# Causal mask of the decay matrices: selects by index on GpSimd in place of a masking product in PSUM

## The chip, the cores and the metric

The kernel runs on one core of a Trainium2 chip. A core has a matrix engine (TensorE, PE in the profile, with its weight loads as PEld), a vector engine (VectorE, DVE), an engine for functions of one operand (ScalarE, ACT), a general engine (GpSimd, POOL) and a queue from which most transfers are issued (SyncE, SP). The metric is the time of the program on the device in microseconds; each kernel is timed in several runs and the median is given.

## The reference

One streaming step of a trunk layer: an input projection, a group of four gated-DeltaNet heads beside a pooling group, an output projection and a SwiGLU feed-forward part, over 2048 prompt frames and 64 frames of a running stream. What the change touches is the decay matrix `gamma` of a chunk, which is lower triangular:

```python
G = jnp.cumsum(g, axis=-1)
lower_incl = idx[:, None] >= idx[None, :]
lower_strict = idx[:, None] > idx[None, :]
gamma = jnp.exp(jnp.where(lower_incl, G[..., :, None] - G[..., None, :], -jnp.inf))
...
Lm = jnp.where(lower_strict, jnp.einsum('bhncd,bhnsd->bhncs', kb, k) * gamma, 0.0)
...
qk = jnp.einsum('bhncd,bhnsd->bhncs', q, k) * gamma
```

`Lm` is then inverted as a unit triangular matrix (`T`), and `T`, `qk` and the decayed keys feed a scan over the chunks.

## The kernel before, in words

The prompt is cut into four blocks of 512 frames; the 64 frames of the running stream ride along with the first. Per block the kernel projects (`pp`, fp32r products of weights split in a high and a low part, `wsp`), runs the heads and the pooling groups, and multiplies with the output projection (`pz`). When the four blocks are through, the feed-forward part runs over all frames in three passes; it is more than half of the time and has none of the changed code.

A head takes a block of 512 frames as four chunks of 128. The class `Front` prepares two chunks at a time: there are 32 fronts for the prompt (4 blocks x 4 heads x 2) and one, `s`, for the running stream, which packs two heads of 64 frames into each 128 x 128 tile. A front does the following, with the line numbers of the kernel before:

- `rowmm` (L1008) puts the running sum G, one row for all partitions, into a PSUM bank `gb`. ScalarE takes its exponential EG from it (tile `TV`); GpSimd copies the last column (`EL`), and VectorE makes `Qd`.
- A bf16 product of an identity `idbf` and a tile `negm` (0 on and above the diagonal, -1e30 below) is added onto the same bank (L1056). For `s` it is `negm2`, which also masks the block where two heads would mix. So it must wait until EG has been read.
- ScalarE takes the exponential of the masked bank with a bias per partition: the decay matrix `Gam`, zero where it is masked. Rows are the earlier frame and columns the later one.
- GpSimd subtracts the identity: `U` (tile `Gst`, L1061) is the decay without its diagonal of ones.
- TensorE multiplies keys with queries and keys (`gr`); VectorE multiplies the results with `U` and with `Gam`, in place. GpSimd adds a scaled identity `idw` to `U`, ScalarE casts it to f16 (`Wh`).
- Seven levels of small f16 products (`py`, `pt`) with level masks `lmask` on VectorE build the inverse; `pf`, `px` refine it once. The scan (`pk`, `po`) follows.

The masks and identities are made once at the start by VectorE, from a DMA of `lmask` (seven level masks and the causal one) and from the constants.

Two things set the order of the work. The program text is only recorded: every engine call becomes an operation with a rank (`Machine.note`), and `Machine.issue` lays all of them out on the five engines by a list schedule, with an estimate of each operation's duration (`Machine.cost`, L147), margins and buffer slots. That order is fixed in the program; on the chip each engine works through its own list and waits on semaphores. All instructions stand under one line, L285, where the recorded call is made, so they are told apart by the names of their tiles. And `Front.all` yields between its steps (`yield LAT_G` and the like), which sets how many products of other work are recorded between two steps of a front.

Of the kernel before, what the change touches and what calls it, by code (L numbers as in the profile page):

```python
# [10 lines left out]
BF16 = mybir.dt.bfloat16  # L11
# [3 lines left out]
ALU = mybir.AluOpType  # L15
# [3 lines left out]
P = 128  # L19
# [3 lines left out]
DEC = 64  # L23
NTOK = SEQ + DEC
C = 128
# [344 lines left out]
def hybrid_kernel(ctx, tc, a, o):  # L370
    nc = machine = Machine(tc.nc)
# [7 lines left out]
    def cost(n, dt):  # L379
        clock["pe"] += n * (1.67e-3 if dt == F32 else 0.427e-3) + 0.005  # L380

    def mm(out, lhsT, rhs, start, stop, **kw):
        nc.tensor.matmul(out, lhsT, rhs, start=start, stop=stop, **kw)
        n = 1
        for d in out.shape[1:]:
            n *= d
        cost(n, rhs.dtype)
# [55 lines left out]
    def pool(name, where=ctx, early=False, behind=False, **kw):  # L443
        return Pool(machine, where.enter_context(tc.tile_pool(name=name, bufs=1, **kw)), early, behind)
# [7 lines left out]
    cp1, gp = pool("cp1", p1, True), pool("gp", p1, True)  # L452
# [24 lines left out]
    for lo, n in S0:  # L477
        for i in range(2):
            nc.sync.dma_start(out=x0[i][:, :, lo : lo + n],
                              in_=a["xT"][4 * i : 4 * i + 4, :, lo : lo + n].rearrange("k p t -> p k t"))  # L480
# [35 lines left out]
    for j in range(NBLK):  # L516
        win = [("win", m) for m in range(21)]
        base = len(plan)
# [409 lines left out]
    ident, convw, onw, psc = names["ident"], names["convw"].rearrange("p (m t) -> p m t", t=4), names["onw"], names["psc"]  # L928
# [11 lines left out]
    selp = cp1.tile([P, 4, 1], F32R, tag="selp", name="selp")  # L940
    nc.vector.tensor_copy(selp, names["sel"].unsqueeze(2))
    lm_f = gp.tile([P, 2, YW], F32, tag="Yqk", name="lm_f", bufs=NY).rearrange("p i n -> p (i n)")[:, :1024].rearrange("p (i n) -> p i n", i=2).rearrange("p i (l n) -> p (i l) n", n=P)
    nc.sync.dma_start(out=lm_f, in_=a["lmask"])
    lmask = cp1.tile([P, 8, P], F16, tag="lmask", name="lmask")
    nc.vector.tensor_copy(lmask[:, :7], lm_f[:, :7])
    negm = cp1.tile([P, P], BF16, tag="negm", name="negm")
    nc.vector.tensor_copy(negm, lm_f[:, 7])

    negm2 = cp1.tile([P, P], BF16, tag="negm2", name="negm2")
    nc.vector.tensor_copy(negm2, lm_f[:, 7])  # L950
    nc.vector.memset(negm2[:DEC, DEC:], -1e30)
    id16 = cp1.tile([P, P], F16, tag="id16", name="id16")
    nc.vector.tensor_copy(id16, ident)
    idw = cp1.tile([P, P], F16, tag="idw", name="idw")
# [1 line left out]
    pm = bank(0, "pm")  # L956
    mm(pm[:, :P], lmask[:, 0], id16, start=True, stop=True)
    nc.scalar.copy(lmask[:, 7], pm[:, :P])
    idbf = cp1.tile([P, P], BF16, tag="idbf", name="idbf")
    nc.vector.tensor_copy(idbf, ident)  # L960

    def history(B, t, x, at, step, keep):

# [9 lines left out]
    def bc(t, nch, n):  # L973
        return t.unsqueeze(1).to_broadcast([t.shape[0], nch, n])
# [4 lines left out]
    class Front:  # L979
# [43 lines left out]
        def all(self):  # L1023
            tag, chunk = self.tag, self.chunk
# [13 lines left out]
            for c in range(2):  # L1038
# [8 lines left out]
            gb = self.ps(f"gb_{tag}")  # L1047
# [5 lines left out]
            Qd = self.Qd = gt([P, 2, C], F32, "Qd", NOUT)  # L1053
            tt(Qd, self.Yqk[:, 0, self.off : self.off + 2 * C].rearrange("p (c n) -> p c n", n=C), EG, ALU.mult)

            mm(gb[:, : 2 * C], idbf, bc(negm2 if self.h is None else negm, 2, C), start=False, stop=True,  # L1056
               skip_group_check=True)
            Gam = self.QKG = gt([P, 2, C], F32, "Gam", NOUT)
            for c in range(2):
                act(Gam[:, c], gb[:, c * C : (c + 1) * C], AF.Exp, bias=self.fall()[:, c : c + 1])  # L1060
            U = lev(F32, "Gst")  # L1061
            nc.gpsimd.tensor_tensor(out=U, in0=Gam, in1=bc(ident, 2, C), op=ALU.subtract)
            yield LAT_G
            ps = self.ps(f"gr_{tag}")
            for c in range(2):
# [52 lines left out]
            for c in range(2):  # L1118
                for i in range(2):
                    mm(px[:, c * C : (c + 1) * C], FF[:, i, c], V[:, c], start=c == i == 0, stop=i == 1,  # L1120
                       skip_group_check=c > 0)
# [416 lines left out]
    for k in (4, 5, 6, 7, 0, 1, 2, 3):  # L1538
        t = wpool.tile([P, 512], F32, tag="xc", name=f"od{k}", bufs=XBUFS["xc"])
# [23 lines left out]
    for nm in FH[3:]:  # L1563
        t = f2.tile([P, 4, 2, N2], F32R, tag=f"h{nm}", name=f"hB{nm}")
        hq[nm] = [t[:, k] for k in range(4)]
    fill = Chain(load_h(0, FH[3:]))
# [194 lines left out]
    for op in order:  # L1761
        b = op[1]
        if op[0] == "gu":
# [18 lines left out]
            if f == NF - 1 and b + 1 < NB2:  # L1782
                nxt.finish()
                fill = Chain(load_h(b + 1, FH))
# [63 lines left out]
def _layout(inp):  # L1848
    import numpy as np

    g = {k: np.asarray(v) for k, v in inp.items()}
    f32 = np.float32
    r = {}
    xp, xs = g["x_prompt"][0], g["x_sample"][0]
    xa = np.concatenate([xp[: PB[0]], xs, xp[PB[0] :]], axis=0)
    r["xT"] = xa.T.reshape(KT, P, NTOK)
    col = lambda w: w.reshape(-1, P).T
    r["nw"] = np.concatenate([col(g["norm1_w"][0]), col(g["norm2_w"][0]), col(g["normf_w"])], axis=1)
    w = g["w_in"][0]

    def tiles(w):
        K, M = w.shape
        return w.reshape(K // P, P, M // P, P).transpose(2, 1, 0, 3).reshape(M // P, P, K)

    ab = np.zeros((D, P), f32)
    ab[:, 0:4] = w[:, 2048:2052]
    ab[:, 32:36] = w[:, 2052:2056]
    ab[:, 64:] = ab[:, :64]
    cols = [ab]
    for h in range(NH):  # L1870
        for i in range(4):
            cols.append(w[:, (4 * i + h) * P : (4 * i + h + 1) * P])
    cols.append(w[:, 2056:])
    r["win"] = tiles(np.concatenate(cols, axis=1))
    r["wout"] = tiles(g["w_out"][0])
    r["wg"], r["wu"] = tiles(g["w_gate"][0]), tiles(g["w_up"][0])

    wd, f0, rows = g["w_down"][0].reshape(NF, P, D), 0, []
    for G in FGROUPS:
        rows += [f0 + i for i in (*range(0, G, 2), *range(1, G, 2))]  # L1880
        f0 += G
    r["wd"] = tiles(wd[rows].reshape(NF * P, D))
    c = {}
    c["convw"] = g["conv_w"][0].reshape(4, 12, P).transpose(2, 1, 0)
    c["onw"] = g["onorm_w"][0].reshape(P, 1)
    c["psc"] = col(g["pool_scale"][0])
    c["poolw"] = g["pool_w"][0].transpose(2, 0, 1)
    c["alog"] = np.zeros((P, 1), f32)
    c["alog"][0:4, 0] = g["a_log"][0]
    c["dtb"] = np.zeros((P, 1), f32)  # L1890
    c["dtb"][0:4, 0] = g["dt_bias"][0]
    c["sconv"], c["spool"] = np.zeros((P, 12, 2, 3), f32), np.zeros((P, 4, 2, HP), f32)
    c["sconv"][:, :, 1] = g["state_conv"][0, 0].T.reshape(12, P, 3).transpose(1, 0, 2)
    c["spool"][:, :, 1] = g["state_pool"][0, 0].T.reshape(4, P, HP).transpose(1, 0, 2)
    c["sdelta"] = g["state_delta"][0, 0].transpose(1, 0, 2)

    c["sgn"] = np.ones((P, 1), f32)
    c["sgn"][32:64] = c["sgn"][96:] = -1.0
    c["ident"] = np.eye(P, dtype=f32)
    i = np.arange(P)  # L1900
    lm = np.zeros((P, 8, P), f32)
    for l in range(7):
        s = 1 << l
        lm[:, l, :] = (i[:, None] == i[None]) * 1.0 - ((i[:, None] // (2 * s) == i[None] // (2 * s)) & (i[:, None] // s > i[None] // s))
        lm[:, l, :] /= WSCALE
    lm[:, 7, :] = np.where(i[None] >= i[:, None], 0.0, -1e30)
    r["lmask"] = lm
    z = np.zeros((P, 12), f32)
    for t in range(3):
        for h in range(4):  # L1910
            z[32 * t + h, 4 * t + h] = 1.0
    c["sel12"] = z
    z = np.zeros((P, 4), f32)
    for h in range(4):
        z[h, h] = 1.0
        z[32 + h, h] = 1.0
    c["sel"] = z
    z = np.zeros((P, 4, 16), f32)
    for gi, win in enumerate(WIN):
        z[:, gi, :] = 1.0 / np.minimum(win, np.arange(16) + 1)  # L1920
    c["pcnt"] = z
    r["consts"] = np.concatenate([c[nm].reshape(P, w).astype(f32) for nm, w in CONSTS], axis=1)
    return {k: np.ascontiguousarray(v) for k, v in r.items()}
# [32 lines left out]
```

## Time and profile before

| | |
|---|---|
| median of 3 runs | 2296.41 us (2295.73 to 2298.98) |
| span of the profiled execution | 2295.8 us |
| instructions | 41549 |
| data moved | 536.96 MB |
| first part, with the heads | about 0 to 905 us |
| feed-forward part | from there to the end |

The span is what the profile shows of one execution, from its first to its last instruction. Matrix products are pipelined: the row of a product gives its length from entry to exit, and the next one starts earlier than it ends. Names such as `gb_p` are tiles, with `_p` for the prompt and `_s` for the running stream.

### The profile page before, as it was taken

Reading aid. Unit: us, or ns where it says so; the run is one execution under the profiler, and the core shown is the slowest. Engines: PE = TensorE matmul, PEld = TensorE weight load, DVE = VectorE, ACT = ScalarE, POOL = GpSimd, SP = SyncE. Lnnn points to the kernel's source line nnn. Section 1 sums busy time; section 2 is a strip of 40 time slices with the busy share of each in tenths; the row PEclk is TensorE's granted clock in tenths of the full one; section 3 lists DMA queues with packets and bytes.
Section 4 is the critical chain, followed back from the end, with each engine's and each line's share of the span. In section 5 each row is a group of like instructions: output and inputs, shape, how many; then the busy total and the mean of one; then the engine's idle time right before and its main releaser. Section 6 shows DMA issues by size and latency. Waiting matters only on the chain.

```text
span 2295.8 us, 41549 instructions
## 1 busy us (share of the span) xinstructions
PE 2271.8 (99%) x14518; PEld 2132.1 (93%) x14518; DVE 1711.3 (75%) x3129; ACT 1342.1 (58%) x3039; POOL 833.4 (36%) x893
## 2 busy tenths in 40 slices
PE   8999999999999999999999999999999999999998
PEld 8898898888787888999999999999999999999998
DVE  8989876685678896788888786866667768666576
ACT  6986866684769864565446366554334574353344
POOL 3425342453247450565434236622111453010112
PEclk9999999999999999999999999999999999999999
DMA  8755586578476767866776578778765776666653
GB/s 295 263 182 193 199 294 234 191 238 277 159 245 232 212 212 254 304 247 247 272 260 238 185 264 292 248 266 302 234 198 199 263 271 230 209 216 224 210 195 103
DMA packets 256514, 536.96 MB, mean 234 GB/s; under 512 B 30000, under 2 KB 94000, under 8 KB 256304
## 3 DMA queue, kind: packets, MB, share of 16 engines
q1 hardware_dynamic: 255728, 533.58, 69.3%
q8 instruction: 114, 1.87, 0.3%
q14 instruction: 96, 0.79, 0.1%
q10 hardware_dynamic: 576, 0.72, 0.1%
HBM read 403.62 MB, written 130.58 MB: 233 GB/s over the span
## 4 chain that ended last, share of the span: by engine, by line
PE 88%; DVE 5%; DMA 3%; ACT 2%; issue 1%; POOL 1%; SPq 0%; DVEq 0%; POOLq 0%; ACTq 0%
PE px L285 21%; PE pp L285 17%; PE pz L285 13%; PE py L285 10%; PE dx L285 8%; PE dy L285 4%; PE d L285 3%; PE dz L285 2%; PE pk_p L285 2%; PE pt_p L285 2%; PE gr_p L285 1%; DVE y L285 1%; PE py_p L285 1%; DVE h L285 1%; DMA hpd<-xt 1%
## 5 line engine op out<-in xcount | busy, mean ns | idle before, releaser
L285 PE MATMUL pp<-h,wsp 128*128 128x512 f32 (+1 forms) x2480 | 547.9, 364 | 10.0 <-DVE wsp L285 10.0
L285 PEld LDWEIGHTS pp<-h,wsp 128*128 128x128 f32 x2480 | 401.4, 189 | 58.2 <-ACT wsp L285 9.2
L285 ACT CAST ws<-wr 128x512 fp32r<-128x512 f32 x198 | 122.1, 618 | 166.7 <-PE dx L285 55.2
L285 DVE TENSOR_TENSOR ws<-wr,ws 128x512 fp32r<-128x512 f32 x198 | 173.4, 879 | 30.9 <-ACT ws L285 27.1
L285 POOL TENSOR_TENSOR q<-hr,hr 128x352 f32<-128x352 f32 x52 | 58.0, 1116 | 369.6 <-DVE hr L285 366.8
L285 ACT CAST wsd<-wrd 128x512 fp32r<-128x512 f32 (+1 forms) x120 | 62.6, 526 | 174.8 <-PE dx L285 66.8
L285 DVE TENSOR_TENSOR y<-y,dx 128x352 f32<-128x352 f32 x240 | 121.8, 517 | 57.0 <-PE dx L285 56.0
L285 PE MATMUL pz<-op,wsp 128*128 128x288 f32 (+1 forms) x768 | 163.0, 353 | 0.0
L285 PE MATMUL px<-hA,ws 128*128 128x352 f32 x792 | 145.2, 322 | 0.0
L285 ACT ACTIVATE hr<-g 128x352 f32<-128x352 f32 x132 | 65.6, 497 | 133.7 <-DVE g L285 133.5
L285 PE MATMUL py<-hA,wsS 128*128 128x352 f32 x792 | 141.5, 322 | 2.0 <-DMA wsS<-gS 1.6
L285 PE MATMUL py<-hB,wsS 128*128 128x352 f32 x792 | 141.7, 322 | 0.0
L285 PE MATMUL pz<-hB,ws 128*128 128x352 f32 x792 | 141.0, 322 | 0.0
L285 ACT CAST TV_p<-pt_p 128x512 f16<-128x512 f32 x192 | 110.4, 589 | 49.6 <-PE pt_p L285 49.2
L285 PE MATMUL px<-hA,wsS 128*128 128x352 f32 x792 | 138.5, 322 | 0.0
L285 PE MATMUL px<-hBT,wsS 128*128 128x352 f32 x792 | 137.9, 322 | 0.2 <-ACT g L285 0.2
L285 PE MATMUL px<-hBT,ws 128*128 128x352 f32 x792 | 137.7, 322 | 0.0
L285 PEld LDWEIGHTS pz<-op,wsp 128*128 128x128 f32 x768 | 120.9, 188 | 12.1
L285 PEld LDWEIGHTS py<-hA,wsS 128*128 128x128 f32 x792 | 129.4, 188 | 2.6 <-DMA wsS<-gS 1.9
L285 PEld LDWEIGHTS px<-hA,ws 128*128 128x128 f32 x792 | 130.0, 188 | 0.1
L285 PE MATMUL dy<-hq,wsdS 128*128 128x352 f32 x672 | 129.6, 322 | 0.0
L285 PEld LDWEIGHTS py<-hB,wsS 128*128 128x128 f32 x792 | 129.4, 188 | 0.0
(697 smaller groups left out, 5777.2 us busy)
## 6 DMA issues: line engine op xcount, KB each, us to landing
wsS<-gS SPq DMA_DIRECT2D x176, 512.0 KB, 4.5
wsp<-wnd SPq DMA_DIRECT2D x126, 512.0 KB, 3.8
gS<-wsS SPq DMA_DIRECT2D x88, 512.0 KB, 4.9
wsdS<-dsd SPq DMA_DIRECT2D x88, 512.0 KB, 4.4
wr<-in_wg_dram SPq DMA_DIRECT2D x132, 256.0 KB, 3.5
wnd<-wsp SPq DMA_DIRECT2D x42, 512.0 KB, 5.0
wrd<-in_wd_dram SPq DMA_DIRECT2D x68, 256.0 KB, 2.7
xd<-x2d SPq DMA_DIRECT2D x96, 176.0 KB, 4.1
```

The costliest lines, as they stand in the source:

```text
L285: getattr(getattr(self.nc, op.eng), name)(*args, **kw)
```

## The change

The masking product, its two mask tiles and the bf16 identity are left out, and the load of the masks brings seven tiles in place of eight. ScalarE takes the exponential of the unmasked bank. In place of the subtraction, GpSimd makes two selects by index: `U` takes `Gam` where the column is above the row and 0 elsewhere (so no diagonal), and then `Gam` is rewritten in place with 0 where the column is below the row. For the front `s` each select is followed by a memset of the block where the two heads would mix.

```diff
-    nc.sync.dma_start(out=lm_f, in_=a["lmask"])
+    nc.sync.dma_start(out=lm_f[:, :7], in_=a["lmask"])
     lmask = cp1.tile([P, 8, P], F16, tag="lmask", name="lmask")
     nc.vector.tensor_copy(lmask[:, :7], lm_f[:, :7])
-    negm = cp1.tile([P, P], BF16, tag="negm", name="negm")
-    nc.vector.tensor_copy(negm, lm_f[:, 7])
-
-    negm2 = cp1.tile([P, P], BF16, tag="negm2", name="negm2")
-    nc.vector.tensor_copy(negm2, lm_f[:, 7])
-    nc.vector.memset(negm2[:DEC, DEC:], -1e30)
...
-    idbf = cp1.tile([P, P], BF16, tag="idbf", name="idbf")
-    nc.vector.tensor_copy(idbf, ident)
...
-            mm(gb[:, : 2 * C], idbf, bc(negm2 if self.h is None else negm, 2, C), start=False, stop=True,
-               skip_group_check=True)
             Gam = self.QKG = gt([P, 2, C], F32, "Gam", NOUT)
             for c in range(2):
                 act(Gam[:, c], gb[:, c * C : (c + 1) * C], AF.Exp, bias=self.fall()[:, c : c + 1])
             U = lev(F32, "Gst")
-            nc.gpsimd.tensor_tensor(out=U, in0=Gam, in1=bc(ident, 2, C), op=ALU.subtract)
+            for t, op in ((U, ALU.is_gt), (Gam, ALU.is_ge)):
+                nc.gpsimd.affine_select(out=t, in_=Gam, pattern=[[0, 2], [1, C]], compare_op=op, fill=0.0, base=0, channel_multiplier=-1)
+                if self.h is None:
+                    nc.gpsimd.memset(t[:DEC, :, DEC:], 0.0)
...
-    lm = np.zeros((P, 8, P), f32)
+    lm = np.zeros((P, 7, P), f32)
...
-    lm[:, 7, :] = np.where(i[None] >= i[:, None], 0.0, -1e30)
```

The layout of the lists is made anew from the changed operations, so the first part is ordered differently throughout; behind it the lists agree. Three places follow. In VectorE's list at the start of the program, where the constants are made, the kernel before has this (`wsp_3_147` is the split of projection weights, `consts` the folded pooling weights):

```order
L285 CAST selp<-consts 128x4
L285 CAST lmask<-lm_f 128x896
L285 CAST negm<-lm_f 128x128
L285 CAST negm_159<-lm_f 128x128
L285 MEMSET negm_159 64x64
L285 CAST id_160<-consts 128x128
L285 TENSOR_SCALAR idw<-consts 128x128
L285 CAST idbf<-consts 128x128
L285 TENSOR_SCALAR consts<-consts 128x128
L285 TENSOR_TENSOR wsp_3_147<-wrp_3_146,wsp_3_147 128x512
```

and the changed kernel this:

```order
L285 CAST selp<-consts 128x4
L285 CAST lmask<-lm_f 128x896
L285 CAST id_158<-consts 128x128
L285 TENSOR_SCALAR idw<-consts 128x128
L285 TENSOR_SCALAR consts<-consts 128x128 x4
L285 TENSOR_TENSOR wsp_3_147<-wrp_3_146,wsp_3_147 128x512
```

Four operations are gone ahead of the split, and the three later ones of the four on `consts` have moved ahead of it.

In TensorE's list at the first two fronts (`p_0_0` and `p_0_1` of the first head, first block) the kernel before has:

```order
L285 MATMUL gb_p_0_0_231<-Ghl_169,selp 128x256
L285 MATMUL pp_7_0_254<-h_0_116,wsp_8_204 128x288 x10
L285 MATMUL pp_7_288_255<-h_0_115,wsp_8_202 128x288 x2
L285 LDWEIGHTS idbf
L285 MATMUL gb_p_0_0_231<-negm,idbf 128x256
L285 MATMUL po_p_0__409<-Qd_p_0_0_233,Sp 128x128
L285 MATMUL gb_p_0_1_240<-Ghl_169,selp 128x256
L285 MATMUL pp_7_288_255<-h_0_115,wsp_8_202 128x288 x10
L285 MATMUL pp_7_288_255<-h_0_116,wsp_8_204 128x288 x2
L285 LDWEIGHTS idbf
L285 MATMUL gb_p_0_1_240<-negm,idbf 128x256
L285 MATMUL gr_p_0_0_245<-Yqk_0_178 128x256 x2
```

and the changed kernel:

```order
L285 MATMUL gb_p_0_0_228<-Ghl_166,selp 128x256
L285 MATMUL pp_7_0_247<-h_0_116,wsp_8_201 128x288 x11
L285 MATMUL pp_7_288_248<-h_0_115,wsp_8_199 128x288 x4
L285 MATMUL gr_p_0_0_249<-Yqk_0_175 128x256 x2
L285 MATMUL po_p_0__409<-Qd_p_0_0_230,Sp 128x128
L285 MATMUL gb_p_0_1_237<-Ghl_166,selp 128x256
```

The two mask products and their weight loads are gone, and `gr` of the first front stands 15 `pp` products behind its row product, where it stood behind 24 of them, two masks and two further products. In ScalarE's list at the same place the exponential EG (`TV_p_0_0`) and the decay matrix now stand side by side, with nothing of other work between:

```order
L285 ACTIVATE TV_p_0_0_227<-gb_p_0_0_228 128x256
L285 ACTIVATE Gam_p_0_0_231<-gb_p_0_0_228,EC_167 128x128 x2
L285 ACTIVATE ktl_p_0_1_234,kn_p_0_1_233<-ptk_p_0_1_235 128x128
L285 ACTIVATE ktl_p_0_1_234<-ptk_p_0_1_235,EC_167 128x128 x2
L285 ACTIVATE kn_p_0_1_233<-kn_p_0_1_233,epsc 128x2
```

In the kernel before the `ktl`, `kn` and one `E` row stood between the two. GpSimd's list at these fronts had:

```order
L285 COPY EL_p_0_0_232<-TV_p_0_0_230 128x2
L285 TENSOR_TENSOR Gst_p_0_0_235<-Gam_p_0_0_234,consts 128x256
L285 COPY EL_p_0_1_241<-TV_p_0_1_239 128x2
L285 TENSOR_TENSOR Gst_p_0_1_244<-Gam_p_0_1_243,consts 128x256
L285 TENSOR_TENSOR Gst_p_0_0_235<-Gst_p_0_0_235,idw 128x256
```

and has:

```order
L285 COPY EL_p_0_0_229<-TV_p_0_0_227 128x2
L285 AFFINE_SELECT Gst_p_0_0_232<-Gam_p_0_0_231 128x256
L285 AFFINE_SELECT Gam_p_0_0_231<-Gam_p_0_0_231 128x256
L285 TENSOR_TENSOR Gst_p_0_0_232<-Gst_p_0_0_232,idw 128x256
L285 COPY EL_p_0_1_238<-TV_p_0_1_236 128x2
L285 AFFINE_SELECT Gst_p_0_1_241<-Gam_p_0_1_240 128x256
L285 AFFINE_SELECT Gam_p_0_1_240<-Gam_p_0_1_240 128x256
```

Each subtraction has become two selects, and the addition of `idw` to the first front has moved ahead of the second front's rows.

## The prediction

> **What bounds the kernel now.** I read the page first, for the engine on which the time is spent, and then the stages, to see where that engine has to wait.
>
> ```profile
> span 2295.8 us, 41549 instructions
> PE 2271.8 (99%) x14518; PEld 2132.1 (93%) x14518; DVE 1711.3 (75%) x3129; ACT 1342.1 (58%) x3039; POOL 833.4 (36%) x893
> PE 88%; DVE 5%; DMA 3%; ACT 2%; issue 1%; POOL 1%; SPq 0%; DVEq 0%; POOLq 0%; ACTq 0%
> ```
>
> The reader is to see one engine that is never free: TensorE (PE) is busy 99% of the span, 88% of the chain that ended last is its own work, and its clock is granted in full (the column 1.00 of the next rows). VectorE (DVE) is three quarters full, GpSimd (POOL) a little over a third. So a product taken off TensorE is worth its place in TensorE's queue, and a microsecond added to GpSimd costs nothing until somebody waits for it.
>
> The changed code runs in the first part alone (the last mask product starts at 812.9 us). The stages of that part, in the columns PE, PEld, DVE, ACT, POOL, then the granted clock, the share of the DMA engines and GB/s:
>
> ```profile
> 0.00:50.00 50.00, 39.71 (x282) 39.05 (x283) 39.68 (x90) 33.93 (x78) 19.75 (x32) 1.00 0.83 294
> 50.00:100.00 50.00, 49.71 (x391) 46.15 (x390) 46.41 (x92) 43.03 (x112) 20.59 (x27) 1.00 0.72 252
> 200.00:250.00 50.00, 48.98 (x318) 38.49 (x317) 45.81 (x94) 39.15 (x104) 23.26 (x31) 1.00 0.62 209
> 400.00:500.00 100.00, 100.00 (x621) 81.61 (x620) 76.81 (x151) 72.88 (x181) 48.96 (x68) 1.00 0.60 207
> ```
>
> TensorE has gaps at the start (10.3 us, before and around its first weights) and about 1 us at 200 to 250 us; in the rows between and behind it has next to none. In the first 300 us VectorE is the next engine, with 46.41 and 45.81 of 50 us. GpSimd has half its time free in each of these rows. From 900 us on the order of instructions is the same in both kernels, and nothing there enters the sum.
>
> **The change, part by part.** *The mask products.* There are 32 of them on heads of the prompt and one on the sample, and one weight load for each.
>
> ```profile
> L285 PE MATMUL gb_p<-negm,idbf x32: 269/282/286, 62.7 to 812.9; 128*128 128x256 bf16 x32
> 62.72 0.28 PE L285 MATMUL gb_p<-negm,idbf 128*128 128x256 bf16 x1
> 62.84 0.39 PE L285 MATMUL po_p__409<-Qd_p,Sp 128*128 128x128 f32 x2
> 64.79 0.28 PE L285 MATMUL gb_p<-negm,idbf 128*128 128x256 bf16 x1
> 64.91 1.03 PE L285 MATMUL gr_p<-Yqk 128*128 128x256 f32 x4
> 699.07 0.28 PE L285 MATMUL gb_p<-negm,idbf 128*128 128x256 bf16 x1
> 699.10 0.48 PE L285 MATMUL pp<-h,wsp 128*128 128x512 f32 x1
> 699.42 0.28 PE L285 MATMUL gb_p<-Ghl,selp 128*128 128x256 f32 x1
> 699.53 1.77 PE L285 MATMUL pp<-h,wsp 128*128 128x512 f32 x7
> 701.15 0.28 PE L285 MATMUL gb_p<-negm,idbf 128*128 128x256 bf16 x1
> ```
>
> The 282 ns are the length of one from entry to exit; products overlap, so what one costs is the distance from its start to the next start. That is 0.12 us twice (62.72 to 62.84, 64.79 to 64.91). At 699.07 the next product starts 0.03 us later but then holds the queue 0.32 us, while the seven behind it take (701.15 - 699.53) / 7 = 0.23 each: 0.03 + 0.09 = 0.12 again. For 31 of the 33 that makes 31 x 0.12 = **3.7 us**. The other two stand together:
>
> ```profile
> 201.60 0.31 PE L285 MATMUL gb_p<-Ghl,selp 128*128 128x256 f32 x1
> 201.98 0.27 PE L285 MATMUL gb_s<-negm,idbf 128*128 128x256 bf16 x1
> 202.44 0.27 PE L285 MATMUL gb_p<-negm,idbf 128*128 128x256 bf16 x1 [0.19 <-ACT TV_p L285]
> 202.70 0.49 PE L285 MATMUL pk_p<-vn_p,ktl_p 128*128 128x128 f32 x2
> ```
>
> A mask has to wait until ScalarE (ACT) has read the bank that it adds to (`TV_p`, the exponential EG, is what released the second). From 201.98 to 202.70 TensorE's queue holds nothing but these two: **0.7 us** more.
>
> *The constants.* The two mask tiles and the bf16 identity are made by VectorE at the start, right ahead of a weight split for which TensorE waits:
>
> ```profile
> 18.84 0.97 DVE L285 CAST negm<-lm_f 128x128 bf16<-128x128 f32 x2
> 19.57 0.62 ACT L285 CAST wsp<-wrp 128x512 fp32r<-128x512 f32 x1 [0.50 <-DMA wnd<-wsp]
> 19.88 0.11 DVE L285 MEMSET negm<- 64x64 bf16 x1
> 20.62 0.83 DVE L285 CAST idbf<-consts 128x128 bf16<-128x128 f32 x1
> 21.57 2.50 DVE L285 TENSOR_TENSOR wsp<-wrp,wsp 128x512 fp32r<-128x512 f32 x2
> 22.92 1.98 PE L285 MATMUL pp<-h,wsp 128*128 128x288 f32 x13 [0.78 <-DVE wsp L285]
> 24.06 0.66 DVE L285 TENSOR_SCALAR consts<-consts 128x128 f32<-128x128 f32 x3
> ```
>
> VectorE loses 0.97 + 0.11 + 0.83 = 1.91 us there. The new order puts the three small products of 24.06 (0.66 us) into that place, so the split can start 1.25 us sooner, at 20.3. What is late next is ScalarE's cast of the same weights, done at 19.57 + 0.62 = 20.2: it does not hold the split up. The whole wait of TensorE, 0.78 us, goes: **0.8 us**. The load of the masks, which becomes an eighth smaller, I cost at nothing: no wait of the trace ends on it, and a smaller one lands no later.
>
> *The selects.* One subtraction on GpSimd becomes two selects per front (33 subtractions, 66 selects, and two small memsets for the sample). No row shows a select, so I bound it from both sides:
>
> ```profile
> L285 POOL MEMSET wsp<- 128x256 f32 x2 | 0.6, 312 | 0.3 <-POOLq L1938 0.3
> L285 POOL TENSOR_TENSOR Gst_p<-Gam_p,consts x32: 719/742/1242, 63.9 to 814.3; 128x256 f32<-128x256 f32 x32
> L285 POOL TENSOR_TENSOR pw<-pw 128x591 f32<-128x591 f32 x1 | 1.9, 1852 | 0.1
> ```
>
> Writing 256 columns with nothing read took 0.31 us; the subtraction on the same tile took 0.74 in the middle, up to 1.24; the longest elementwise row of the list, more than twice as wide, took 1.85. A select reads one tile and writes one, with an index to compare in between. I take **0.75 us**, the row that it replaces, and keep 0.31 and 1.85 as ends. GpSimd's work then grows by 33 x (1.5 - 0.74) = 25 us, in a part where it is free half of the time. What counts is the chain. For the first front:
>
> ```profile
> 60.92 0.39 PE L285 MATMUL gb_p<-Ghl,selp 128*128 128x256 f32 x1 [0.28 <-ACT ktl_p L285]
> 61.14 1.74 PE L285 MATMUL pp<-h,wsp 128*128 128x288 f32 x12
> 61.36 0.40 ACT L285 ACTIVATE TV_p<-gb_p 128x256 f32<-128x256 f32 x1
> 63.18 0.68 ACT L285 ACTIVATE Gam_p<-gb_p,EC 128x128 f32<-128x128 f32 x2
> 63.93 0.74 POOL L285 TENSOR_TENSOR Gst_p<-Gam_p,consts 128x256 f32<-128x256 f32 x1 [1.66 <-ACT Gam_p L285]
> 66.22 0.60 DVE L285 SCALAR_TENSOR_TENSOR Gst_p<-gr_p,kn_p,Gst_p 128x128 f32<-128x128 f32 x2
> 66.74 0.41 DVE L285 TENSOR_TENSOR Gam_p<-gr_p,Gam_p 128x256 f32<-128x256 f32 x1
>   DVE Gst_p L285: 0.6, 1
> ```
>
> EG ends at 61.76 and the decay matrix Gam only starts at 63.18, because the mask comes between. In the new order of ScalarE the two stand next to each other: Gam would run 61.76 to 62.44, and the selects, 0.08 us later as at 63.93, end at 62.5 + 0.75 and 62.5 + 1.5 = 64.0. The subtraction now ends at 64.67. So the pair is done sooner than the one it replaces, as long as a select takes under 1.07 us. But the new order also spends this: it puts the products `gr` on TensorE 15 `pp` behind the row product of 60.92, and 12 `pp` took 61.14 to 62.72, 0.132 each: 61.14 + 15 x 0.132 = 63.1, where they stood at 64.91. VectorE multiplied Gam 1.83 us behind `gr` (66.74 - 64.91), so it would now ask for it at 64.9. The second select is in time up to (64.9 - 62.5) / 2 = 1.2 us. The last row, from the waits on this tile, says that VectorE stood once in 32 fronts for GpSimd's subtraction, 0.6 us; behind a late select would stand VectorE's products with the level masks, for which TensorE's next level waits. At 0.75 I cost this at **0.3 us** in all, for the fronts whose `gr` comes closest; with a select of 0.31 it would be nothing.
>
> *A rule to weigh.* The Trainium skill (GPSIMD Engine Reference, 3.1) speaks against this edit: data-dependent branching costs about 12 cycles per element there, while 4.1 calls one-input operations roughly line-rate. By the 1.2 GHz of that page an estimate for 256 columns is 2.6 us by the one and 0.2 us by the other; no row here shows which applies to a select. With the first the sum would turn into the slow rival below, with the second only its 0.3 us would go.
>
> *The sum.* 3.7 + 0.7 + 0.8 - 0.3 = 4.9 us off the profiled execution's 2295.8, that is 2290.9. The median of the runs shown, 2296.41, lies 0.6 above this span, so I predict **2291.5 us**.
>
> **The rivals.** *Given back where VectorE sets the pace.* Cut at 300 us, the view of the mask tiles has this row on prompt heads, and the one of the sample at 202.0:
>
> ```profile
> L285 PE MATMUL gb_p<-negm,idbf x11: 269/282/286, 62.7 to 286.3; 128*128 128x256 bf16 x11
> ```
>
> So 12 of the 33 masks stand where VectorE is busy 46.41 and 45.81 of 50 us. If TensorE reaches VectorE's results sooner there and only waits for them, the 12 slots (1.2 for ten, 0.7 for the pair) and the 0.8 at the start come to nothing: 4.9 - 2.7 = 2.2 us are left, 2294.2. For it speaks that the new order moves `gr` and all that follows on VectorE forward; against it, that the page has only 1 us of idle TensorE at 200 to 250. The Trainium skill (SBUF — State Buffer, section on the two separate sides) adds a reason: a GpSimd operation and a VectorE one with two SBUF inputs exclude each other for their whole length. The subtraction's spread of 719 to 1242 ns above agrees with that, and 25 us more of GpSimd would hold VectorE up a little more often.
>
> *A slow select.* The order is fixed when the program is built, so an engine that is late stops its queue. Above 1.2 us per select the first front's Gam comes late by twice the excess, and the 32 fronts together lose 64 times the excess if TensorE gets all of it. It decides from 1.2 + 4.9 / 64 = 1.3 us on. At 1.45 us, between the slowest subtraction (1.24) and the longest row (1.85), it costs 64 x 0.25 = 16 us: 2296.4 - 4.9 + 16 = 2307.5. For it: no row of a select, and a spread of the subtraction that reaches 1.24. Against it: the middle row is 0.74, and a select reads one input less.
>
> *The change does not do what it says.* The masks could have come back in another form. The order that the front shows has no `idbf` or `negm` left at its places and two selects where the subtraction stood, so I give this 2 in 100; it would be 2296.4.
>
> **How the numbers follow.** Forecast 62 in 100, with a range of its own of 2289.0 to 2294.0; rival on VectorE 20; slow select 16; no change in fact 2. What a measurement of this kernel can tell from no change is about 0.2%, 4.6 us, so faster begins at 2291.8, in the upper middle of the forecast's range: 38 of its 62 lie below it: faster 0.38. The other 24, the 20 of VectorE's rival and the 2 of no change are within 0.2%, less 1 for a VectorE that loses more than it was given: 0.45. Slower is that 1 and the slow select: 0.17. The range: its low end allows 3.5 us beyond the sum, for a cheap select and an order that happens to wait less, 2288.0; its high end takes in the second rival and the slow select up to 1.35 us (64 x 0.15 - 4.9 = 4.7 above 2296.4), 2301.0. Left out are most of the slow select, some 13 in 100, and 6 in 100 below.
>
> **What would show it.** Right: no bf16 product in the list of TensorE; the start of `pp` at 22.92 without its wait for VectorE; TensorE's busy time in 50 to 850 us shorter by about 4 us and no new row in TensorE's waits that ends on VectorE or GpSimd for more than a few tenths; selects of 0.3 to 1.0 us. Wrong: selects above 1.2 us with VectorE's product Gam waiting for GpSimd in most fronts; or stages before 300 us that take as long as now, with new TensorE gaps that VectorE ends; or a moved DMA issue for which TensorE waits, which I have at nothing, as the list of SyncE keeps its loads and only shifts them by a few places.

## The result, and the profile after

The changed kernel takes **2302.39 us** (median of 20 runs, 2298.96 to 2307.96), the kernel before in the same comparison 2297.23 us (20 runs, 2295.73 to 2301.12): a ratio of 1.0020 (95% interval 1.0014 to 1.0027). It is 5 us slower, where 5 us faster was forecast, and it lies above the forecast range (2288.0 to 2301.0). The profiled execution spans 2301.2 us against 2295.8.

The head of the page, of the changed kernel:

```profile
span 2301.2 us, 41494 instructions
PE 2273.9 (99%) x14485; PEld 2128.3 (92%) x14485; DVE 1705.2 (74%) x3125; ACT 1341.3 (58%) x3039; POOL 830.2 (36%) x928
```

The 33 products are gone (14518 to 14485) and VectorE has four operations less. GpSimd has 35 instructions more and is busy *less* than before (833.4). Busy times do not show where 5 us went; the stages do. The same stages as in the prediction, and one of 3.4 us inside the third:

```profile
0.00:50.00 50.00, 40.89 (x289) 40.38 (x290) 39.09 (x89) 34.73 (x81) 18.95 (x33) 1.00 0.84 298
50.00:100.00 50.00, 49.71 (x401) 46.80 (x400) 44.28 (x89) 43.12 (x113) 24.02 (x31) 1.00 0.71 246
200.00:250.00 50.00, 47.92 (x294) 38.22 (x294) 43.91 (x81) 32.41 (x69) 19.95 (x24) 0.97 0.63 205
400.00:500.00 100.00, 98.34 (x604) 78.56 (x602) 74.14 (x149) 71.23 (x176) 44.69 (x68) 1.00 0.60 195
235.50:238.90 3.40, 3.40 (x10) 2.55 (x9) 2.51 (x6) 0.00 (x0) 0.00 (x0) 0.50 0.64 199
```

Up to 100 us the changed kernel is ahead (289 and 401 products in the first two rows, where 282 and 391 stood). At 200 to 250 us it does 24 products fewer than before, TensorE idles 2.1 us instead of 1.0, and the granted clock, 1.00 in every row of before, is 0.97: the last row shows why, 3.4 us at exactly half clock. At 400 to 500 us there is 1.7 us of idle time that was not there. TensorE's first product of the feed-forward part starts at 938.17 us, where it started at 933.03: nearly the whole loss is made before that part.

What TensorE waited for up to 910 us (waiting tile, what ended the wait, us in total, times, longest):

```profile
PE pp L285 <- DVE wsp L285: 9.1, 2, 8.7
PE pc L285 <- DVE Rt L285: 2.0, 3, 1.1
PE pp L285 <- DVE h L285: 1.0, 3, 0.6
PE px_p L285 <- DVE TV1F_p L285: 0.6, 1, 0.6
PE os_p__2169 L285 <- DVE lo_p__2171 L285: 0.5, 1, 0.5
PE pk_p L285 <- DVE Sp L285: 0.5, 1, 0.5
PE pf_s L285 <- ACT TV_s L285: 0.5, 1, 0.5
```

In the kernel before, the first row reads 10.0 and no other row has more than 0.3. Of these rows all but the last end on VectorE, and the largest new one on `Rt`, the running sum that opens each block, for whose products `pc` TensorE stands three times (0.70, 0.24 and 1.07 us).

### The profile page after: what moved, and what is told of

Same layout as the page of the kernel before. It is cut to its first block, busy times and chain, and to the rows that moved or that the text cites. A ratio compares the mean times of both kernels' runs of the same rounds, so it can differ in the third digit from the quotient of the medians.

```text
span 2301.2 us, 41494 instructions
## 1 busy us (share of the span) xinstructions
PE 2273.9 (99%) x14485; PEld 2128.3 (92%) x14485; DVE 1705.2 (74%) x3125; ACT 1341.3 (58%) x3039; POOL 830.2 (36%) x928
## 4 chain that ended last, share of the span: by engine, by line
PE 87%; DVE 6%; DMA 3%; ACT 2%; issue 1%; POOL 0%; SPq 0%; DVEq 0%; ACTq 0%; POOLq 0%
PE px L285 20%; PE pp L285 16%; PE pz L285 13%; PE py L285 10%; PE dx L285 9%; PE dy L285 4%; PE d L285 3%; PE dz L285 2%; PE pk_p L285 2%; PE pt_p L285 2%; PE gr_p L285 1%; DVE y L285 1%; PE py_p L285 1%; DVE h L285 1%; DVE Rt L285 1%
## 5 line engine op out<-in xcount | busy, mean ns | idle before, releaser
L285 PEld LDWEIGHTS px<-hA,wsS 128*128 128x128 f32 x792 | 128.9, 188 | 0.9 <-ACT g L285 0.9
```

The lines of the kernel that those rows point to most:

```text
L285: getattr(getattr(self.nc, op.eng), name)(*args, **kw)
```

## The experiments

The kernel before was timed again beside each group of kernels, and its median moved (2297.23 to 2299.55), so each kernel is compared with the runs of before that were taken beside it. The ratios and intervals are estimated from the runs and are not the quotients of the medians, from which they differ by up to 0.0006. "Old list" is the order of the kernel before, "own" the one laid out from the changed operations with the constants as they were.

| label | work and list | median | before | difference | ratio (95% interval) |
|---|---|---|---|---|---|
| the change | changed, own list | 2302.39 | 2297.23 | +5.2 | 1.0020 (1.0014 to 1.0027) |
| e1_old_order | changed, old list | 2298.78 | 2299.55 | -0.8 | 0.9996 (0.9987 to 1.0005) |
| e3_selects_only | masks and selects, old list | 2298.24 | 2299.55 | -1.3 | 0.9997 (0.9988 to 1.0006) |
| b_lat473 | before, LAT_G 4.73 | 2297.72 | 2299.55 | -1.8 | 0.9998 (0.9989 to 1.0006) |
| a_lat473 | changed, LAT_G 4.73 | 2301.86 | 2299.55 | +2.3 | 1.0012 (1.0004 to 1.0021) |
| n_filled | changed and 33 idle products, own list | 2307.13 | 2299.13 | +8.0 | 1.0035 (1.0022 to 1.0048) |
| n_tv210 | changed, LAT_TV 2.1 | 2297.14 | 2299.13 | -2.0 | 0.9995 (0.9986 to 1.0004) |
| n_g603 | changed, LAT_G 6.03 | 2300.72 | 2299.13 | +1.6 | 1.0009 (1.0001 to 1.0018) |
| b_tv210 | before, LAT_TV 2.1 | 2296.38 | 2299.13 | -2.8 | 0.9987 (0.9978 to 0.9996) |
| n_rtwait | changed, own list, GpSimd waits at `Rt` 1, 2 | 2301.33 | 2298.60 | +2.7 | 1.0010 (1.0001 to 1.0019) |
| n_tv_xd | changed, LAT_TV 2.1, later `xd` | 2294.25 | 2298.60 | -4.4 | 0.9982 (0.9973 to 0.9991) |
| b_tv_xd | before, LAT_TV 2.1, later `xd` | 2297.78 | 2298.60 | -0.8 | 0.9996 (0.9988 to 1.0005) |
| g_tv_xd | changed, list of b_tv_xd | 2293.81 | 2298.60 | -4.8 | 0.9979 (0.9971 to 0.9988) |
| n_rt3 | n_rtwait, and `Rt` 3 | 2299.03 | 2297.90 | +1.1 | 1.0005 (0.9997 to 1.0014) |
| n_best | n_tv_xd, GpSimd waits at `Rt` 2, 3 | 2292.75 | 2297.90 | -5.2 | 0.9978 (0.9969 to 0.9987) |

### Is it the work or the order?

Two theories stood at the start: the selects or the missing masks cost something of themselves, or the new order does. *e1_old_order* makes the whole change but keeps the order of the kernel before: the old operations are laid out as if they were there, and those that the change removes are then not issued. *e3_selects_only* keeps the masks too and replaces only the subtraction.

```diff
+            machine.ghost = True
             mm(gb[:, : 2 * C], idbf, bc(negm2 if self.h is None else negm, 2, C), start=False, stop=True,
                skip_group_check=True)
+            machine.ghost = False
...
-            nc.gpsimd.tensor_tensor(out=U, in0=Gam, in1=bc(ident, 2, C), op=ALU.subtract)
+            for t, op in ((U, ALU.is_gt), (Gam, ALU.is_ge)):
+                nc.gpsimd.affine_select(out=t, in_=Gam, pattern=[[0, 2], [1, C]], compare_op=op, fill=0.0, base=0, channel_multiplier=-1)
```

> The whole change (masks, mask tiles and bf16 identity gone, selects in place of the subtraction), but the lists of all engines laid out as in the kernel before: the removed operations are planned and not issued, the selects stand where the subtraction stood. Theory A, the loss is the new layout of the lists: this kernel keeps the gain, about 2292.5 us (3.7 + 0.7 + up to 0.8 off 2297.2). Theory B, the selects hold VectorE up wherever they stand: about as slow as the changed kernel, 2301 to 2303.

> The masking products stay and the selects take the place of the subtraction, in the old layout of the lists (the selects then find their zeros already there). Theory A: no change, 2296.5 to 2298, since the pair takes 0.8 us where the subtraction took 0.74. Theory B: 2300 or more.

*b_lat473* and *a_lat473* lay out the kernel before and the changed one with `LAT_G = 4.73` in place of 4.53.

> The kernel before with the constant LAT_G at 4.73 in place of 4.53: the same work, another layout of the lists. Theory A1, any new layout of this program comes out a few us worse than the one of before: 2299 to 2305. Theory A2, the layout of the changed kernel is bad for a reason of its own (fronts packed closer): this one stays at 2296 to 2298.

> The changed kernel with LAT_G at 4.73: the same work as the changed kernel, another layout. A1: anywhere between 2292 and 2306, on average 4 to 5 us under other layouts of the kernel before. A2: 2301 to 2304 again.

The selects cost nothing: e3_selects_only is at 0.9997. Their rows in the changed kernel, found under the tiles they write (least, median and greatest ns, first and last start):

```profile
L285 POOL TENSOR_SCALAR_AFFINE_SELECT Gst_p<-Gam_p x32: 399/407/928, 61.3 to 826.1; 128x256 f32<-128x256 f32 x32
L285 POOL TENSOR_SCALAR_AFFINE_SELECT Gam_p<-Gam_p x32: 406/408/997, 61.7 to 826.5; 128x256 f32<-128x256 f32 x32
```

At 0.41 us each, two selects last about as long as the one subtraction (0.74). But e1_old_order gains only 0.8 us, within its uncertainty, which is the number of neither theory, and the changed kernel stays slow in a second order of its own (a_lat473), while the kernel before does not mind its own second order (b_lat473). The 2301.86 us of a_lat473 lie in the range of its theory A2, but the kernel before beside it was 2.3 us slower than beside the change; by the difference, +2.3, it lies between its two theories. So there are two questions: why freed slots bring nothing in the old list, and why the new list costs 5 us.

In e1_old_order TensorE runs ahead of the kernel before up to 500 us. It gives that back at 530 to 570 us (two waits of 0.9 us in all for a load of weights, one of 0.5 for ScalarE) and, the larger part, at 797 to 808 us. One row of VectorE and one of TensorE from there (the recorded call is line 298 in this kernel):

```profile
802.17 0.59 DVE L298 SCALAR_TENSOR_TENSOR xd<-xd,nw,r 128x352 f32<-128x352 f32 x1 [4.54 <-DMA xd<-x2d]
803.74 0.49 PE L298 MATMUL pk_p<-rhs_p,X_p 128*128 128x128 f32 x2 [2.47 <-DVE rhs_p L298]
```

`xd` are rows of the trunk that are loaded to prepare the feed-forward part; the first products on them stand in the last block of the first part, from about 758 us on, the last ones at 1615 us. No head needs them, but VectorE takes its list in order, so while it stands 4.54 us for a late load, everything of the heads behind it stands too. The kernel before stands 3.15 us for a load of `xd` there too, at 804.5, and TensorE has other work meanwhile. In e1_old_order TensorE's clock is then at half for 3.4 us (804.7 to 808.2). e3_selects_only, which keeps the masks, stands there too: in its profile VectorE waits 4.44 us for `xd` (to 806.86) and TensorE 1.91 us behind it, at full clock. So freed slots are not needed for this stall.

### Do freed slots count at all?

*n_filled* takes the changed kernel's lists word for word and puts a product of a mask's size back behind each row product, into the unused half of the bank.

```diff
             self.rowmm(gb)
+            machine.ride = True
+            nc.tensor.matmul(gb[:, 2 * C : 4 * C], id16, bc(lmask[:, 0], 2, C), start=True, stop=True, skip_group_check=True)
+            machine.ride = False
```

> The changed kernel with its lists exactly as they are, and 33 products of TensorE put back where the masks could have stood: right behind each row product, an f16 product of 128 x 128 by 256 columns into the unused half of the same bank, which nobody reads and nobody waits for. Same time on TensorE as a mask (0.12 us each, 3.9 us in all), without the mask's waits. If freed slots shorten the program in this list, as the prediction's sum has it, filling them again costs 3.9 us: about 2306. If TensorE is paced by what it waits for in this list, filling them costs nearly nothing: 2302 to 2303.

It is 8.0 us over the kernel before, 2.8 more than the change, from five runs and with intervals that overlap; in the profiles its feed-forward part starts 3.8 us later than that of the change (942.0 against 938.2). So the slots count in this list, the masks' removal is worth something near what the prediction said, and the new list loses some 8 us elsewhere. *n_tv210*, *n_g603* and *b_tv210* look at other lists (`LAT_TV = 2.1` in place of 2.0, `LAT_G = 6.03` in place of 4.53).

> The changed kernel with LAT_TV 2.1 in place of 2.0: the same operations in another order. Theory of the list (the constants had been chosen for the old operations, and the list that they give for the new ones is a poor one among many): another list is several us better, 2293 to 2298. Theory of the shorter hop (without the mask every front goes from its row product to gr sooner, so every list of the changed operations runs into waits for VectorE): 2300 or more, as the two lists so far (2302.4 and 2301.9).

> The changed kernel with LAT_G 6.03 in place of 4.53, a third other order, in which more of other work is recorded between the steps of a front. Theory of the list: 2293 to 2299, below the two lists so far. Theory of the shorter hop: 2300 or more.

> The kernel before with LAT_TV 2.1: the other side of n_tv210. If the changed operations are worth something once both are laid out by the same new constant, n_tv210 comes out 2 to 5 us below this one. Theory of the list: this one is within 2 us of the kernel before or worse by a few, since nothing is removed; theory of the shorter hop: it is 3 us or more below n_tv210.

Both theories are partly right. One list of the changed operations is 7 us better than the other (+5.2 and -2.0), and lists of the kernel before differ too (0, -1.8, -2.8). But with the same constants the changed operations are not ahead in any of these three pairs: +5.2 against 0, +2.3 against -1.8, -2.0 against -2.8. n_g603 falls on the side of the shorter hop, n_tv210 on the side of the list. b_tv210 meets none of its expectations: it is 2.8 us below the kernel before, and n_tv210 came out 0.8 above it.

Both new lists of the changed operations stall in the last block. In n_g603 it is GpSimd that stands, 5.43 us for a transfer, at a sum on `xd` for the feed-forward part (to 796.92); ScalarE and then TensorE stand behind it, TensorE for 3.56 us, and the half clock follows. In n_tv210 it is VectorE, as in e1_old_order. The profile of n_tv210 is that of the slowest of its eleven runs (2301.19 us, where the median is 2297.14); by their mean granted clock seven of them had no stretch at half clock (0.999; the profiles with such a stretch have 0.9978 to 0.9984, those without 0.9985 to 0.9992). Of n_tv210, VectorE, then TensorE, then the stages on both sides of TensorE's return (PE, PEld, DVE, ACT, POOL, clock, DMA share, GB/s):

```profile
804.35 1.46 DVE L285 SCALAR_TENSOR_TENSOR xd<-xd,nw,r 128x352 f32<-128x352 f32 x1 [2.94 <-DMA wsp<-wnd]
806.07 0.33 DVE L285 SCALAR_TENSOR_TENSOR Sp<-Sp,EL_p,pk_p 128x128 f32<-128x128 f32 x1
806.46 0.59 PE L285 MATMUL pk_p<-Sp,Yqk 128*128 128x128 f32 x2 [2.57 <-DVE Sp L285]
803.20:806.70 3.50, 0.93 (x7) 0.48 (x6) 2.35 (x5) 0.92 (x4) 1.21 (x2) 1.00 0.94 320
806.80:810.00 3.20, 3.20 (x17) 2.54 (x15) 1.35 (x5) 1.30 (x5) 1.14 (x3) 0.50 0.31 102
```

The name of the load in the first row is that of the transfer that ended last in the profile; the operand is `xd`. In the 3.5 us of TensorE's wait the DMA engines are 94% busy, which fits loads that are late because the transfers are full there. `Sp` behind it has nothing to do with `xd`. And behind the gap TensorE runs at half clock, 3.4 us in all, which adds 1.7 us to the 2.6 of the wait.

### The two repairs

*n_tv_xd* and *b_tv_xd* let the layout take the loads of `xd` as landing 2.5 us later, so VectorE's product on them goes further back in its list. This holds for every load of `xd`, those of the feed-forward part too: the lists are others from about 760 us up to 1650 us. *g_tv_xd* is e1_old_order's edit made on the lists of b_tv_xd.

```diff
         late = SLACK if q.eng == "tensor" and p.eng != "sync" and q.order > self.second else 0.0
+        if p.eng == "sync" and q.eng == "vector" and p.tiles and p.tiles[0].startswith("xd"):
+            late += XD
...
+XD = 2.5
-LAT_TV = 2.0
+LAT_TV = 2.1
```

*n_rtwait* aims at the `Rt` waits. The rows of VectorE and GpSimd around the start of the second block, in the changed kernel:

```profile
230.12 2.33 DVE L285 TENSOR_TENSOR_SCAN Rt<-ones,Rt 4x128 f32<-4x128 f32 x4
230.47 0.90 POOL L285 TENSOR_TENSOR prdn<-prdn 128x256 f32<-128x256 f32 x1
231.45 0.73 POOL L285 TENSOR_TENSOR prdn<-consts,prdn 128x256 f32<-128x256 f32 x1
232.25 0.64 POOL L285 TENSOR_TENSOR consts<-prdn,consts 128x256 f32<-128x256 f32 x1
232.48 1.54 DVE L285 TENSOR_SCALAR Rt<-Rt 4x128 f32<-4x128 f32 x4
232.97 0.78 POOL L285 TENSOR_TENSOR consts<-consts 128x256 f32<-128x256 f32 x1
233.03 0.61 PE L285 MATMUL pc<-consts,Rt 128*128 128x12 f32 x4 [0.70 <-DVE Rt L285]
```

and the corresponding ones of the kernel before:

```profile
226.87 1.35 DVE L285 TENSOR_TENSOR_SCAN Rt<-ones,Rt 4x128 f32<-4x128 f32 x4
229.02 0.67 DVE L285 TENSOR_SCALAR Rt<-Rt 4x128 f32<-4x128 f32 x3
229.37 1.01 PE L285 MATMUL pc<-consts,Rt 128*128 128x12 f32 x8
229.63 0.73 POOL L285 TENSOR_TENSOR prdn<-prdn 128x256 f32<-128x256 f32 x1 [2.05 <-DMA prdn<-in_wd_dram]
```

`prdn` are sums of down-projection weights that GpSimd prepares for the feed-forward part. In the kernel before their load lands just behind the running sum; in the changed one they run beside it, and four scans take 2.33 us instead of 1.35. n_rtwait makes GpSimd wait for the last row of `Rt` in blocks 1 and 2 (the second and the third, as blocks are counted from 0) by a copy of one column; in the first part nothing else moves in any engine's list.

```diff
+        if j in RTWAIT:
+            machine.after[RTWAIT[j]] = f"Rt{j}_", tick[64:68], Rt[64:68, YW - 1 : YW]
...
+RTWAIT = {1: "prdn4_0", 2: "prdn8_1"}
```

> The changed kernel with its lists as they are, and two copies of one column on GpSimd that wait for the last row of the running sum (Rt) of blocks 1 and 2, ahead of the sums of down weights (prdn) that ran beside these rows. Theory (VectorE's eight Rt rows take 4.3 us instead of 2.66 because GpSimd's two-input operations run beside them, so TensorE waits 0.95 and 1.10 us at pc, and the first of these waits is followed by 3.4 us of half clock): the rows take 2.7 us, both waits go, with them the half clock at 235 us, and the time is 2 to 4 us below the changed kernel: 1 to 3 us above the kernel before on the same chip. Rival (the waits only move to the next point where VectorE is late): 5 us above the kernel before, as the change itself.

> The changed kernel with LAT_TV 2.1 and a layout that takes the loads of xd (last block, at 770 to 900 us) to land 2.5 us later than before, so that VectorE's product on them stands further back in its list; up to about 770 us the lists are those of n_tv210. Theory (in the last block the transfers set the pace: VectorE stands 2.9 us at xd, TensorE behind it 2.6 us, and the half clock follows): that wait goes, and with it 2 to 4 us of n_tv210's time; 4 to 6 us below the kernel before. Rival (the wait is that of one execution, or comes back behind the next load): as n_tv210, 2 us below the kernel before.

> The kernel before with the same two constants as n_tv_xd. If loads of xd that are late cost the masks' kernel as much: 1 to 3 us below b_tv210, 4 to 5 below the kernel before. If the masks' kernel loses nothing there, as its profile says (3.15 us of VectorE's wait without a wait of TensorE): as b_tv210, 2 to 3 below the kernel before.

> The lists of b_tv_xd, with the masking products and their constants left out of them and the two selects in the subtraction's place: e1_old_order once more, on lists in which xd has 2.5 us more to land. If e1_old_order gained nothing because TensorE, once ahead, stood longer for the late loads and lost the clock there, the freed slots now show: 3 to 4.5 us below b_tv_xd. If freed slots are given back wherever TensorE gets ahead: within 1 us of b_tv_xd.

In n_rtwait the running sum is as fast as in the kernel before, and GpSimd's copy and sum come behind it:

```profile
231.51 1.35 DVE L288 TENSOR_TENSOR_SCAN Rt<-ones,Rt 4x128 f32<-4x128 f32 x4
232.88 0.87 DVE L288 TENSOR_SCALAR Rt<-Rt 4x128 f32<-4x128 f32 x4
233.56 0.96 PE L288 MATMUL pc<-consts,Rt 128*128 128x12 f32 x8
233.88 0.97 POOL L286 COPY tick<-Rt 4x1 f32<-4x1 f32 x1 [1.99 <-DVE Rt L288]
234.93 1.18 POOL L288 TENSOR_TENSOR prdn<-prdn 128x256 f32<-128x256 f32 x1
```

TensorE no longer waits at `pc`, its clock is full from 12 to 2292 us, and 10 of 11 runs have a mean granted clock of 0.999, where 13 of 20 of the changed kernel have 0.998 (a stretch of 3.4 us at half clock takes 0.0007 off the mean; the kernel before, whose profile has none, also has 0.998 in 10 of the 33 runs taken here, so some of its runs may have one). The time falls from +5.2 to +2.7, as the theory had it, though the two intervals overlap.

The other repair goes with a kernel faster than before. n_tv_xd, with the lists of n_tv210 up to about 760 us, is 2.4 us below it, has no wait of TensorE over 0.5 us from 50 to 910 us, and is faster than the kernel before by 0.9 to 2.7 in a thousand. b_tv_xd gains nothing by it. Its second expectation foresaw that, but put it 2 to 3 us below the kernel before; it is 0.8 below, and 2 us above b_tv210. The profiles, one execution each, show where this goes. At the first product of the feed-forward part n_tv_xd is 7.4 us ahead of n_tv210 (930.1 against 937.5), at the last product of the program 5.6 (2285.0 against 2290.6); b_tv_xd is 0.4 ahead of b_tv210 (935.6 against 936.0) and then 0.6 behind (2287.8 against 2287.2). So the later `xd` helps in the first part, and the changed order of the feed-forward part takes 1 to 2 us back. Laid out with these two constants, the changed operations are for the first time ahead of the old ones: -4.4 against -0.8.

And **g_tv_xd against b_tv_xd is the prediction's sum by itself**: the same lists, masks out and selects in, 2297.78 - 2293.81 = 4.0 us. Each of the eleven runs of g_tv_xd (2291.93 to 2296.11) is below each of the eleven of b_tv_xd (2297.08 to 2298.31).

Last, *n_rt3* adds the wait in block 3 (three pooling sums `pw` ran beside that running sum), and *n_best* puts both repairs together (waits in blocks 2 and 3).

```diff
-RTWAIT = {1: "prdn4_0", 2: "prdn8_1"}
+RTWAIT = {1: "prdn4_0", 2: "prdn8_1", 3: "pw2_3_2"}
```

> n_rtwait with a third such copy: GpSimd waits for the Rt rows of block 3 too, ahead of the three pooling sums pw that run beside them (4.2 to 5.2 us for the eight rows instead of 2.66, without a wait of TensorE at pc, but VectorE stays behind afterwards, and TensorE waits 0.5 to 0.7 us for it at 655, 681 and 697 us). Theory (VectorE, late by the stretched rows, costs TensorE the later waits): the waits at 681 and 697 go, 1 us below n_rtwait, 1 to 2 us above the kernel before. Rival (the pooling sums are wanted early, so what they lose comes back): as n_rtwait or a little above, 3 us above the kernel before.

> n_tv_xd with the waits of GpSimd ahead of what runs beside the Rt rows of blocks 2 and 3 (there TensorE waits 0.50 us at pc in block 2, and the rows of block 3 take 5.3 us). Theory: 0.5 to 1.5 us below n_tv_xd, 5 to 6 below the kernel before. Rival: as n_tv_xd, 4.4 below it.

n_rt3 is at +1.1 in time, as its theory said, but not by the steps it named: the `Rt` rows do fall to 2.66 us (the eight lengths added up) and the wait at 681 us goes, yet one of 0.5 us stands at 686 in its place, and the one at 697 stays. Against n_rtwait the 1.6 us are within the uncertainty of both. Against the change the two intervals just touch, at 1.0014. In n_best the wait at `pc` of block 2 stays (0.45 us), and the gain over n_tv_xd, 0.8 us, can't be told from none. At 2292.75 us it is the fastest kernel measured, 0.9978 (0.9969 to 0.9987) of the kernel before.

## Why the prediction was wrong, point by point

- **The mask products, 3.7 us and 0.7 for the pair: near as a price.** The whole sum of 4.9, constants and selects included, came to 4.0 us in one unchanged list (g_tv_xd against b_tv_xd), and to 0.8 in the other (e1_old_order); products of their size put back into the changed list cost 2.8 us (n_filled).
- **The constants, 0.8 us: right in kind, half in size.** TensorE's wait did not go, it shrank from 0.78 to 0.39 us:

```profile
22.40 1.85 PE L285 MATMUL pp<-h,wsp 128*128 128x288 f32 x12 [0.39 <-DVE wsp L285]
```

  The split started at 21.06 instead of 20.3, because the small products on `consts` ahead of it took 1.98 us for four, where the prediction had 0.66 for three from another place. The first block's `pc` came 1.1 us sooner than before, but between all profiled executions this point varies from 42.2 to 44.0 us, so no more than a part of it can be claimed.
- **The selects, 0.75 us each: 0.41, too dear by almost half**, without effect, since 0.3 us was all that they were charged. VectorE's products on `Gst_p` waited for GpSimd 0.6 us in all, once for each of the two selects, as they did once for the subtraction. The slow select did not happen. The rule of 12 cycles per element (the Trainium skill, GPSIMD Engine Reference, 3.1) does not hold for this operation; the 0.2 us estimated from line rate (4.1) is nearer, and half of what was measured.
- **The step that failed: the new order, costed at those 0.3 us.** The text ahead of the prediction said that the first part is ordered differently throughout, and the prediction followed only what that does to a front's own chain (`gr`, Gam, the selects). That chain held. What the new order did to operations which the change does not touch was put at nothing: TensorE's other waits were taken over from the old list as if it were the same. By g_tv_xd and n_filled this omission is worth 8 to 9 us: +5.2 measured, against -2.8 to -4.0 for the work alone (by e1_old_order, where the work alone shows -0.8, it is 6). In its place the runs showed TensorE waiting 2.0 us at `pc` for a running sum that weight sums on GpSimd had stretched, and 1.7 us lost by half clock; with GpSimd held back at three of these running sums +5.2 became +1.1.
- **The rival on VectorE had the engine, the reason and part of the place, and the wrong limit.** It said that before 300 us TensorE would wait for VectorE, that GpSimd would hold VectorE up, and priced it at most at what had been gained, 2294.2, with 1 chance in 100 left for more. An order can lose more than it was given, and the waits did not end at 300 us: 1.07 us at 457, and about 0.5 each at 442, 658, 684 and 700. And the operation that held VectorE up was not a select but the weight sums. The stretched rows agree with the exclusive lock of VectorE and GpSimd that the prediction cited from the Trainium skill (SBUF — State Buffer, section on the two separate sides): scans with two inputs took 2.33 us for four instead of 1.35 beside GpSimd's sums. A further section of that page (Who interferes with whom) counts `tensor_scalar` in a 2-port mode among the operations that contend, which would cover the `TENSOR_SCALAR` rows (1.54 us for four instead of 0.87); which mode they ran in, no run here shows.
- **The half clock was in no step.** The changed kernel loses 1.7 us by it (3.4 us at half) behind the wait at `pc`; it is not in the profiles of the kernel before, b_tv_xd, n_rtwait or g_tv_xd. The changed kernel's runs agree: the 13 with a mean clock of 0.998 have a median of 2302.70 us, the 7 with 0.999 one of 2301.02.

What is shown: that the order and not the work costs the time (+5.2 in its own list, -0.8 and -4.8 in two old ones), the work's worth in the list of b_tv_xd, the running sum's share of the loss (+5.2 to +1.1 with three waits added, at the edge of what the intervals tell), and that the late `xd` product stands behind the stall of n_tv210's profiled execution. How much of the 2.4 us between n_tv210 and n_tv_xd is this stall is not shown, since the same constant also reorders the feed-forward part and by their mean clock most runs of n_tv210 did not have the half clock. What is argued only: that the same stall ate e1_old_order's gain. Its profile shows it, but g_tv_xd differs from it in `LAT_TV` and in the order of the feed-forward part as well. What stays open: why the changed operations in their own list are still 1 us above the kernel before with the running sums mended, 4 to 5 us above what the work is worth. Single waits of 0.5 us for `Sp`, `TV1F_p`, `h` and one load are left there, but they were not taken away one by one.

## What to carry to other kernels

Where a program lays out its lists from the operations themselves, an edit is two edits, the work and the order, and they are measured apart: issue the new work in the old list, in more than one of them (here one gave 0.8 us and another 4.0), and put idle work of the old size into the new one. In an in-order queue, what is not urgent but late (a load for a later part) holds up what is urgent: give such operations more time in the layout than the median load takes, and measure it, since here it paid for the changed operations alone. Look at which elementwise work of GpSimd falls beside VectorE's short serial rows; it costs most where TensorE waits for them.

## What the hardware showed that was not expected

- A short gap can halve TensorE's clock. In n_tv210 a wait of 2.57 us and in e1_old_order one of 2.47 was followed by 3.41 us at half clock. In the changed kernel two waits of 0.70 and 0.24 us at `pc` were, in a stretch of 3.4 us in which TensorE counts as busy for 2.45. The first row is this stretch, the second one of the same length that ends with the wait of 1.07 us at 457 us:

```profile
232.10:235.50 3.40, 2.45 (x18) 2.05 (x18) 3.30 (x8) 1.18 (x5) 1.50 (x3) 1.00 0.40 149
453.95:457.36 3.41, 2.34 (x15) 1.68 (x14) 3.38 (x7) 0.91 (x2) 2.67 (x4) 1.00 0.87 287
```

  The second is the less busy one, and no half clock followed it, so this count does not tell which gap is followed by half clock. One difference is in the rows: some 1.2 us of the first stretch are the eight `pc` products, of 12 columns each. Whether that is the reason, no run here shows. The Trainium skill (TensorE: Matmul & The Clock Gate, Part 1) gives such a window as 3413 ns, free-running, and the length agrees to the nanosecond in every case; it lets the clock fall after an idle window, while here a window that was 72% busy by the profile was enough.
- A select by index over 128 x 256 f32 took 0.41 us on GpSimd and 1.00 us at most, about half of a two-input operation on the same tile (0.74).
